# Expert borders of a routed SwiGLU: four scatter products and half a gathering in five PSUM banks, gates applied in the adding, float32 first products, groups of 32

## The chip, the cores and the metric

One core of a Trainium2 chip runs the whole program. The metric is device time in microseconds, median of several runs: 1387.23 us for the kernel before (three runs, 1385.8 to 1388.72). TensorE (PE) multiplies, VectorE (DVE) and ScalarE (ACT) do element work and move results out of PSUM, GpSimd (POOL) fills memory, SyncE (SP) issues the weight transfers.

## What is computed

A two-layer decoder trunk on 256 tokens of width 1024, all in float32. The second layer ends in eight expert SwiGLUs of hidden width 3584; each token goes to its two best experts.

```
logits = xf @ router
top_v, top_i = lax.top_k(logits, 2)
gates = softmax(top_v)
for e in range(8):
    y = y + gate[:, e] * ((silu(xf @ wg[e]) * (xf @ wu[e])) @ wd[e])
x = layer_norm(alpha * x + y)
```

The experts hold 8 x 44 MB of weights, which all pass through the chip once.

## The kernel before

Attention, the dense channel mixer and the router take the first 440 us or so and are not touched. The rest, function `moe`, goes through the experts in the order 3, 0, 1, 4, 5, 6, 7, 2 (ORDER). I number the places in this order e0 to e7.

**Expert bodies.** How many tokens an expert has is known only at run time. `tc.Switch` (line 1206) jumps, on every engine, into one of six bodies (CLASSES): up to 32 tokens, 64, 64 + 32, 128, 128 + 32, 128 + 128. A group of tokens that is computed together is called an arm (class `Part`). The trace shows by the shapes which bodies run: e0 32, e1 128 + 32, e2 64, e3 64 + 32, e4 64, e5 and e6 64 + 32, e7 32. A 128-token arm multiplies in three fp32r products of high and low halves (`mm3`, lines 920 to 922), for which ACT makes the high half (808) and DVE the low half (809) of tokens and weights. Smaller arms multiply in float32 (972 for gate and up, 1024 for down); a float32 matmul leaves two matmul records in the trace, an fp32r one leaves one.

**Weights.** The 42 blocks of 1 MB of an expert (16 gate, 14 up and down parts in turn) go through 17 half buffers. SP issues the transfer of block q + 17 when PE has finished block q (`done`, `fetch`, lines 852 and 857). SP too has six bodies, and goes through the jumps.

**Border between two experts.** In the body's end: `p_.end()` copies the results from PSUM to `hd` (1040, by DVE and ACT in turn), and `pick(0)` gathers the first half of the next expert's tokens, transposed, into `xg`: 8 matmuls with a 0/1 matrix `oh` (867) and a copy (1053, DVE). Then every engine jumps out of the body. The shared piece follows: `pick(1)` (8 matmuls, copy by ACT), a new `oh` that holds the gates (877, DVE), `scatter`, that is four matmuls (908) through the two `tr` banks of PSUM with four DVE adds into `acc` (911), and `shares_of`, which turns the gate matrix for the next expert (889, copy by ACT 890). Then every engine jumps into the next body. `ahead` gives a branch hint, to PE behind the last down product, to ACT behind pick(1), to DVE behind the gate matrix. For the tokens beyond 128 (e1's second arm) the body's start gathers them by full 128-column products (867, copies 1065), and its end scatters them (908, before `pick(0)`). PSUM has eight banks: four `acc`, two `mm`, two `tr`.

The order of instructions on an engine comes from a scheduler that follows data and the edges of `issue_after`; a body's `by_turns` sets how the two arms alternate.

## Time and profile before

| | |
|---|---|
| median of three runs | 1387.23 us |
| the profiled execution | 1387.88 us, its span 1386.2 us |
| PE busy | 1288.0 us (93%) |
| DVE, ACT busy | 483.6 us, 386.1 us |
| read from HBM | 424.32 MB |
| mean granted PE clock | 0.968 |

A row of the windows view gives a stretch of the span, its length, the busy time of each engine with the number of its records, the granted PE clock as a share of full speed, the busy share of the 16 DMA engines and GB/s. A row of the timeline gives start, length, engine, line, operation, output<-input, shape, number of records, and in brackets the engine's idle time before it with what ended it; `issue` means that no wait shows, as when an engine fetches code.

### The profile page before, as it was taken

How to read it: one execution, taken by the hardware profiler on the slowest of the kernel's cores; microseconds unless marked ns; L12 is line 12 of the kernel's file. 1: busy time of each engine (PE TensorE's matmuls, PEld its weight loads, DVE VectorE, ACT ScalarE, POOL GpSimd, SP SyncE). 2: the span in 40 equal slices, each digit the busy share in tenths (PEclk: the TensorE clock that was granted, in tenths of full speed). 3: DMA queues.
4: the chain of work that ended last, by engine and by line, in shares of the span. 5: the costliest groups of instructions: out<-in, count | busy, mean ns of one | idle time of the engine just before them, and what ended most of it. 6: DMA issues, size and time to landing. Idle time of an engine off the chain costs nothing.

```text
span 1386.2 us, 23696 instructions
## 1 busy us (share of the span) xinstructions
PE 1288.0 (93%) x10058; PEld 826.5 (60%) x10058; DVE 483.6 (35%) x786; ACT 386.1 (28%) x690; POOL 32.6 (2%) x51
## 2 busy tenths in 40 slices
PE   8999999999999966999999989998989998999874
PEld 7978999998877624677753333344343454334532
DVE  4688455566767203666751010001010001000102
ACT  5484444444664102556630000000000000000001
POOL 1010000000010000000000000000000000000000
PEclk9999999999999977999999999999999999999977
DMA  9427455554348899977757999999998999999796
GB/s 332 179 92 283 166 191 190 191 182 161 122 152 314 351 408 404 379 274 272 286 204 278 402 405 402 401 408 402 403 406 344 410 402 398 405 399 388 297 402 259
DMA packets 134056, 427.94 MB, mean 309 GB/s; under 512 B 8343, under 2 KB 14487, under 8 KB 133836
## 3 DMA queue, kind: packets, MB, share of 16 engines
q1 hardware_dynamic: 132764, 421.69, 79.2%
q0 software_dynamic: 1072, 3.71, 0.7%
q8 instruction: 90, 1.47, 0.4%
q14 instruction: 130, 1.06, 0.2%
HBM read 424.32 MB, written 1.06 MB: 307 GB/s over the span
## 4 chain that ended last, share of the span: by engine, by line
PE 81%; DMA 10%; issue 3%; DVE 2%; ACT 2%; SPq 1%; POOL 0%; DVEq 0%; ACTq 0%; POOLq 0%
PE mm L972 19%; PE acc L1024 13%; PE acc L972 7%; PE mm L324 4%; PE mm L326 4%; PE mm L325 4%; PE acc L324 4%; PE acc L325 4%; PE acc L326 3%; DMA piece<-in_moe_w_gate_dram 3%; DMA piece<-in_moe_w_up_dram 3%; DMA piece<-in_moe_w_down_dram 3%; PE tr L908 2%; PE mm L920 2%; PE tr L867 2%
## 5 line engine op out<-in xcount | busy, mean ns | idle before, releaser
L972 PE MATMUL mm<-piece,xg 128*64 128x512 f32 (+3 forms) x2048 | 290.5, 483 | 21.7 <-DMA piece<-in_moe_w_up_dram 10.4
L972 PEld LDWEIGHTS mm<-piece,xg 128*64 128x64 f32 (+1 forms) x2048 | 116.2, 129 | 174.6 <-issue 129.6
L1024 PE MATMUL acc<-piece,hT 128*32 128x256 f32 (+1 forms) x1752 | 199.9, 468 | 14.2 <-DMA piece<-in_moe_w_down_dram 13.3
L288 DVE TENSOR_TENSOR wl<-piece,wh 128x1024 fp32r<-128x1024 f32 (+4 forms) x128 | 140.2, 1102 | 89.2 <-ACT wh L286 86.6
L1024 PEld LDWEIGHTS acc<-piece,hT 128*32 128x32 f32 (+1 forms) x1752 | 75.2, 122 | 127.9 <-issue 85.4
L286 ACT ACTIVATE wh<-piece 128x1024 fp32r<-128x1024 f32 (+4 forms) x128 | 122.1, 960 | 86.2 <-PE acc L325 48.0
L324 PE MATMUL mm<-xTh,wl 128*128 128x256 f32 x448 | 126.6, 283 | 0.0
L325 PE MATMUL mm<-xTh,wh 128*128 128x256 f32 x448 | 125.7, 281 | 0.0
L326 PE MATMUL mm<-xTl,wh 128*128 128x256 f32 x448 | 125.7, 281 | 0.0
L990 ACT ACTIVATE hT<-tr 128x256 f32<-128x256 f32 (+2 forms) x43 | 17.9, 444 | 379.3 <-PE tr L997 301.0
L809 DVE TENSOR_TENSOR wl<-piece,wh 128x1024 fp32r<-128x1024 f32 (+1 forms) x88 | 97.8, 1127 | 48.3 <-ACT wh L808 32.1
L983 DVE TENSOR_TENSOR hd<-hd,mm 128x512 f32<-128x512 f32 (+2 forms) x34 | 20.0, 589 | 247.6 <-PE mm L972 247.5
L808 ACT ACTIVATE wh<-piece 128x1024 fp32r<-128x1024 f32 (+1 forms) x88 | 85.7, 983 | 58.0 <-PE mm L921 35.1
L983 DVE TENSOR_TENSOR h<-h,acc 128x256 f32<-128x256 f32 (+1 forms) x16 | 6.2, 388 | 233.6 <-PE acc L972 233.6
L324 PEld LDWEIGHTS mm<-xTh,wl 128*128 128x128 f32 x448 | 84.7, 189 | 0.2
L325 PEld LDWEIGHTS mm<-xTh,wh 128*128 128x128 f32 x448 | 84.5, 189 | 0.2
L326 PEld LDWEIGHTS mm<-xTl,wh 128*128 128x128 f32 x448 | 84.5, 189 | 0.0
L972 PE MATMUL acc<-piece,xg 128*32 128x256 f32 (+1 forms) x1472 | 74.7, 353 | 0.0
L972 PEld LDWEIGHTS acc<-piece,xg 128*32 128x32 f32 x1472 | 43.6, 110 | 36.5 <-issue 15.8
L981 ACT ACTIVATE hd<-mm 128x512 f32<-128x512 f32 (+2 forms) x34 | 17.5, 522 | 154.7 <-PE tr L997 109.9
L867 PE MATMUL tr<-oh,x_sb 128*128 128x128 f32 x288 | 41.6, 304 | 13.1 <-DVE oh L877 6.8
L908 PE MATMUL tr<-hd,sc 128*128 128x512 f32 (+1 forms) x64 | 40.3, 752 | 14.0 <-ACT xg L1053 10.3
(421 smaller groups left out, 1683.7 us busy)
## 6 DMA issues: line engine op xcount, KB each, us to landing
piece<-in_moe_w_gate_dram SPq DMA_DIRECT2D x108, 1024.0 KB, 16.9
piece<-in_moe_w_up_dram SPq DMA_DIRECT2D x104, 1024.0 KB, 18.3
piece<-in_moe_w_down_dram SPq DMA_DIRECT2D x104, 1024.0 KB, 14.9
piece<-in_ffn_w_gate_dram SPq DMA_DIRECT2D x5, 2048.0 KB, 7.9
piece<-in_ffn_w_up_dram SPq DMA_DIRECT2D x5, 2048.0 KB, 8.6
piece<-in_ffn_w_down_dram SPq DMA_DIRECT2D x5, 2048.0 KB, 11.2
piece<-in_w_in_dram SPq DMA_DIRECT2D x4, 2048.0 KB, 11.6
piece<-in_w_o_dram SPq DMA_DIRECT2D x4, 2048.0 KB, 8.4
```

What stands on the lines that cost most here:

```text
L286: hi = act.activation(h, src, AF.Copy)
L288: return hi, dve.tensor_sub(lo, src, h.bitcast(F32))
L324: pe.matmul(ps, lt[1], rt[0], start=start, stop=False)
L325: pe.matmul(ps, lt[0], rt[0], start=False, stop=False)
L326: pe.matmul(ps, lt[0], rt[1], start=False, stop=stop)
L808: act.activation(h, src, AF.Copy)
L809: dve.tensor_sub(lo, src, h.bitcast(F32))
L867: pe.matmul(tp[:, j * P:(j + 1) * P], src[:, t, (j0 + j) * P:(j0 + j + 1) * P], oh[:, t], start=t == 0, stop=t == 1)
L908: pe.matmul(ps, sc[:n, t * P:(t + 1) * P], hd[:n, hf], start=not total, stop=last or not total)
L920: pe.matmul(ps, lt[1], rt[0], start=start, stop=False)
L972: pe.matmul(ps[g * self.n:(g + 1) * self.n, :b], self.tokens(k), v[:, k - k0, g * w + j * b:g * w + (j + 1) * b], **at)
L1024: self.latest = pe.matmul(y[g * self.n:(g + 1) * self.n, c:c + w], self.hidden(j0 + j), v[:, j, i * w:(i + 1) * w], **at)
```

## The change

**Border.** The gates leave the 0/1 matrix: `oh` stays a 0/1 matrix, is turned inside the body behind `pick(0)` (`places_of`), and the gate is a factor in the adding (one `scalar_tensor_tensor` for each of the four sums). In the shared piece `bring` puts the four scatter products into four banks (two `tr`, two `acc`), `pick(1)` goes into an `mm` bank, and the four adds follow. `pick(0)` and the turning stand behind the last down product. Only PE gets a branch hint, behind them. e7, which no shared piece follows, makes its gate matrix in its own body.

**128-token arms.** The first four of eight row blocks of the first gate product use raw float32 `xg` and raw weights; tokens are split only when the fifth comes.

**Beyond 128.** With 32 such tokens, gathering, turning and scattering go in four groups of 32 rows or columns (`pick_few`, `scatter_few`), the gathering behind the first arm's first products; before the last down the arms' order is reversed, so that the small arm ends first.

```diff
-    def picked(src, oh, j0):
-
-        tp = bank("tr")
+    latest = {}
+
+    def picked(src, oh, j0, kind="tr"):
+
+        tp = bank(kind)
         for j in range(4):
             for t in range(2):
-                pe.matmul(tp[:, j * P:(j + 1) * P], src[:, t, (j0 + j) * P:(j0 + j + 1) * P], oh[:, t],
-                          start=t == 0, stop=t == 1)
+                ins = pe.matmul(tp[:, j * P:(j + 1) * P], src[:, t, (j0 + j) * P:(j0 + j + 1) * P], oh[:, t],
+                                  start=t == 0, stop=t == 1)
+        latest["pick"] = ins
...
-    def onehot(dst, e, off, weight):
+    def onehot(dst, e, off, weight, n=P):
 
         for t in range(2):
-            ins = dve.tensor_scalar(dst[:, t], iota[:, off:off + P], pos[:, t, e:e + 1], weight[:, t, e:e + 1],
-                                    op0=ALU.is_equal, op1=ALU.mult)
-        return ins
-
-    def shares(sc, e, off):
-
-        onehot(oh, e, off, gate)
-        shares_of(sc)
-
-    def shares_of(sc):
+            dve.tensor_scalar(dst[:, t].rearrange("p (g n) -> p g n", n=n),
+                              iota[:, off:off + n].unsqueeze(1).to_broadcast([P, P // n, n]),
+                              pos[:, t, e:e + 1], weight[:, t, e:e + 1], op0=ALU.is_equal, op1=ALU.mult)
+
+    def shares(sc, e, off, n=P):
+
+        onehot(oh, e, off, gate, n)
+        places_of(sc)
...
+    def bring(sc, e):
+
+        pss = [[bank(k) for _ in range(2)] for k in ("tr", "acc")]
+        for t in range(2):
+            for hf in range(2):
+                pe.matmul(pss[t][hf], sc[:, t * P:(t + 1) * P], hd[:, hf], start=True, stop=True)
+        return lambda: [dve.scalar_tensor_tensor(acc[:, t, HS[hf]], pss[t][hf], gate[:, t, e:e + 1], acc[:, t, HS[hf]],
+                                                 op0=ALU.mult, op1=ALU.add) for t in range(2) for hf in range(2)]
...
-                self.x = [part("xgh"), part("xgl")]
-                for k in range(0, 1024, 256):
-                    split_into(*[t[:, k:k + 256] for t in self.x], x[:, k:k + 256])
-                self.h, self.hT = h_all, [part("hT"), part("hTl")]
+                self.x, self.h, self.hT = None, h_all, [part("hT"), part("hTl")]
...
+                if self.parts and k < 4 and self.x is None:
+
+                    for j, ps in enumerate(self.ps):
+                        pe.matmul(ps, xg[:, k * P:(k + 1) * P], v[:, k - k0, j * 512:(j + 1) * 512], **at)
+                    continue
                 if self.parts:
+                    if self.x is None:
+                        self.x = [part("xgh"), part("xgl")]
+                        for q in (4, 6, 0, 2):
+                            split_into(*[t[:, q * P:(q + 2) * P] for t in self.x], xg[:, q * P:(q + 2) * P])
...
+    def pick_few(src, w, tmp, to):
+
+        n = 32
+        tp = bank("tr")
+        for t in range(2):
+            for g in range(4):
+                pe.matmul(tp[g * n:(g + 1) * n, :w], oh[:, t, :n], src[:, t, g * w:(g + 1) * w],
+                          start=t == 0, stop=t == 1)
+        act.copy(tmp[:, :w], tp[:, :w])
+        tp = bank("tr")
+        for c in range(0, w, P):
+            pe.transpose(tp[:, c:c + P], tmp[:, c:c + P], ident)
+        act.copy(to, tp[:, :w])
+
+    def scatter_few(sc, y):
+
+        n = 32
+        pss = [bank(k) for k in ("mm", "mm", "tr", "tr")]
+        for t in range(2):
+            for g, ps in enumerate(pss):
+                gs = slice(g * n, (g + 1) * n)
+                pe.matmul(ps[:, t * S:(t + 1) * S], sc[gs, t * P:(t + 1) * P], y[gs], start=True, stop=True)
+        for g, ps in enumerate(pss):
+            o = acc[:, :, g * S:(g + 1) * S]
+            dve.tensor_add(o, o, ps.rearrange("p (t n) -> p t n", t=2))
...
+                    if p_ in to_pick:
+                        to_pick.remove(p_)
+                        pick_beyond(p_)
...
+            shares(mine, e, 0)
...
+        turn[:] = parts[::-1]
         down(len(ws) - 1)
-        if not final:
-            ahead(i + 1, turn[0].latest)
         for p_ in beyond:
-            p_.end()
-            scatter(sc2, p_.n, total)
+            if few and not final:
+                act.copy(p_.h, p_.y[0][:, :S])
+                scatter_few(sc2, p_.h)
+            else:
+                p_.end()
+                if final:
+                    scatter(sc2, p_.n, total)
+                else:
+                    bring_weighted(sc2, p_.n)
...
+            return
+        with tc.issue_after(latest["down"].ins):
             pick(0)
+            turned = places_of(sc2)
+        ahead(i + 1, turned, latest["pick"])
...
-    def ahead(i, ins):
-
-        with tc.issue_after(ins.ins):
-            tc.switch_hint({ins.ins.engine: kinds[ORDER[i]]}, len(CLASSES), f"expert{i}")
...
+    def ahead(i, *behind):
+
+        with ExitStack() as s:
+            for ins in behind:
+                s.enter_context(tc.issue_after(ins.ins))
+            tc.switch_hint({pe.engine: kinds[ORDER[i]]}, len(CLASSES), f"expert{i}")
...
-            ahead(i, pick(1))
-            ahead(i, onehot(oh, e, 0, gate))
-            scatter(backs[(i - 1) % 2], P)
-            shares_of(backs[i % 2])
+            add = bring(backs[(i - 1) % 2], ORDER[i - 1])
+            pick(1, "mm")
+            add()
```

**PE at a border.** First the program before, from the end of a body (the last in the text, all end alike) through the shared piece to the first row of the next body for 32 tokens; line 867 is a pick, 908 the scatter, 889 the turning, 972 the gate product.

```order
L867 MATMUL tr<-oh,x_sb 128x128 x8
L1206 UNCONDITIONAL_BRANCH
L867 MATMUL tr<-oh,x_sb 128x128 x8
L908 MATMUL tr<-hd,sc_4567 128x512 x4
L889 MATMUL tr<-ident,oh 128x128 x2
L173 TENSOR_LOAD kind
L1206 SWITCH_STRIDE
L1206 ISA x2
L1194 BRANCH_PREFETCH_HINT
L972 MATMUL mm<-piece,xg 32x256 x32
```

Now the same place after; 869 is a pick, 893 the turning, 919 the scatter.

```order
L869 MATMUL tr<-oh,x_sb 128x128 x8
L893 MATMUL tr<-ident,oh 128x128 x2
L1249 SWITCH_STRIDE
L1249 ISA
L1249 BRANCH_PREFETCH_HINT
L1277 UNCONDITIONAL_BRANCH
L919 MATMUL tr<-hd,sc_4567 128x512 x2
L919 MATMUL acc<-hd,sc_4567 128x512 x2
L869 MATMUL mm<-oh,x_sb 128x128 x8
L173 TENSOR_LOAD kind
L1277 SWITCH_STRIDE
```

The turning has moved ahead of the jump, the hint behind it; the scatter stands before the second pick and uses four banks in place of two.

**PE at the start of the body for 128 + 32 tokens, e1.** Before: 867 gathers the tokens beyond 128, 920 to 922 are the three fp32r products, the first ones on row block 0.

```order
L867 MATMUL tr<-oh,x_sb 128x128 x16
L920 MATMUL mm<-wh,xgl 128x512
L921 MATMUL mm<-wh,xgh 128x512
L922 MATMUL mm<-wl,xgh 128x512
L920 MATMUL mm<-wh,xgl 128x512
L921 MATMUL mm<-wh,xgh 128x512
```

After: 976 are the float32 products of row blocks 0 to 3, 1078 and 1083 gather and turn in groups of 32, 930 to 932 are fp32r products of row block 4, 989 is the small arm.

```order
L976 MATMUL mm<-piece,xg 128x512 x8
L1078 MATMUL tr<-x_sb,oh 32x256 x8
L930 MATMUL mm<-wh,xgl 128x512
L931 MATMUL mm<-wh,xgh 128x512
L932 MATMUL mm<-wl,xgh 128x512
L1083 MATMUL tr<-ident,h_11742 128x128 x2
L930 MATMUL mm<-wh,xgl 128x512
L931 MATMUL mm<-wh,xgh 128x512
L932 MATMUL mm<-wl,xgh 128x512
L989 MATMUL acc<-piece,x_11741 32x256 x32
```

The gathering has moved behind eight products that need neither it nor a split.

**PE at the end of that body.** Before: 1024 is the small arm's last down, 908 the scatter of the tokens beyond 128.

```order
L922 MATMUL acc<-wl,hT 128x512
L1024 MATMUL acc<-piece,hT_11867 32x256 x7
L1177 SWITCH_STRIDE
L1177 ISA
L1177 BRANCH_PREFETCH_HINT
L908 MATMUL tr<-hd,sc_4566 128x512 x4
L867 MATMUL tr<-oh,x_sb 128x128 x8
L1206 UNCONDITIONAL_BRANCH
```

After: the large arm's fp32r products (932) come last, 1093 is the scatter in four groups.

```order
L932 MATMUL acc<-wl,hT 128x512
L1093 MATMUL mm<-h_11742,sc_4566 128x256 x2
L1093 MATMUL tr<-h_11742,sc_4566 128x256 x2
L1093 MATMUL mm<-h_11742,sc_4566 128x256 x2
L1093 MATMUL tr<-h_11742,sc_4566 128x256 x2
L869 MATMUL tr<-oh,x_sb 128x128 x8
L893 MATMUL tr<-ident,oh 128x128 x2
L1249 SWITCH_STRIDE
```

The small arm is now out of the way before the large arm's last products, and its scatter needs half the columns at a time.

More of the change, by code (lines that the diff above doesn't have):

```diff
@@ L901, in moe, with scatter @@
     backs = [mc.tile([P, S], F32, name=f"sc{n}") for n in range(2)]
-    def scatter(sc, n, total=None, last=False):
+    def scatter(sc, n, total, last=False):
         for t in range(2):
             for hf in range(2):
-                ps = total[t][hf] if total else bank("tr")
-                pe.matmul(ps, sc[:n, t * P:(t + 1) * P], hd[:n, hf], start=not total, stop=last or not total)
-                if not total:
-                    o = acc[:, t, HS[hf]]
-                    dve.tensor_add(o, o, ps)
+                pe.matmul(total[t][hf], sc[:n, t * P:(t + 1) * P], hd[:n, hf], start=False, stop=last)
+    def bring(sc, e):
[5 more added lines that the diff above has]
+                                                 op0=ALU.mult, op1=ALU.add) for t in range(2) for hf in range(2)]
     def split(src):
@@ L953, in tokens @@
             if self.off == P:
-                return self.x[:, k * self.n:(k + 1) * self.n]
+                c0 = k * P if self.n == P else k % 2 * P + k // 2 * self.n
+                return self.x[:, c0:c0 + self.n]
             return self.x[:, k * P + self.off:k * P + self.off + self.n]
@@ L1019, in down @@
                     for hf in range(2):
-                        self.latest = mm3(self.y[hf], self.hidden(j0 + j), [x[:, HS[hf]] for x in s], **at)
+                        latest["down"] = mm3(self.y[hf], self.hidden(j0 + j), [x[:, HS[hf]] for x in s], **at)
                     continue
@@ L1023, in down @@
                     y, g, c = self.result(i)
-                    self.latest = pe.matmul(y[g * self.n:(g + 1) * self.n, c:c + w], self.hidden(j0 + j),
-                                            v[:, j, i * w:(i + 1) * w], **at)
+                    latest["down"] = pe.matmul(y[g * self.n:(g + 1) * self.n, c:c + w], self.hidden(j0 + j),
+                                               v[:, j, i * w:(i + 1) * w], **at)
         def result(self, i):
@@ L1049, in moe, with pick, bring_weighted @@
                [(P, 0, True, (A, A), 2), (P, P, False, (TR, TR), 2)]]
-    def pick(q):
-        return (act.copy if q else dve.tensor_copy)(xg[:, q * 512:(q + 1) * 512], picked(x_sb, oh, 4 * q))
+    def pick(q, kind="tr"):
+        (act.copy if q else dve.tensor_copy)(xg[:, q * 512:(q + 1) * 512], picked(x_sb, oh, 4 * q, kind))
+    def pick_few(src, w, tmp, to):
[20 more added lines that the diff above has]
+            dve.tensor_add(o, o, ps.rearrange("p (t n) -> p t n", t=2))
+    def bring_weighted(sc, n):
+        for t in range(2):
+            for hf in range(2):
+                ps, o = bank("tr"), acc[:, t, HS[hf]]
+                pe.matmul(ps, sc[:n, t * P:(t + 1) * P], hd[:n, hf], start=True, stop=True)
+                dve.tensor_add(o, o, ps)
     def expert(i, cls, hT0, mine, sc2):
@@ L1059, in expert, with pick_beyond @@
         beyond = [p_ for p_ in parts if p_.off == P]
-        for p_ in beyond:
+        few = bool(beyond) and beyond[0].n < P
+        def pick_beyond(p_):
             onehot(oh, e, P, route.maskf)
-            w = 4 * p_.n
-            for src, j0, to in ((x_sb, 0, p_.x[:, :w]), (x_sb, 4, p_.x[:, w:2 * w]), (hd, 0, p_.hT[0][:, :w])):
+            if few:
+                pick_few(x_sb, 256, p_.h, p_.x)
+                if i == 0:
+                    pick_few(hd, P, p_.h, p_.hT[0][:, :P])
+                return
+            for src, j0, to in ((x_sb, 0, p_.x[:, :512]), (x_sb, 4, p_.x[:, 512:]), (hd, 0, p_.hT[0][:, :512])):
                 if src is x_sb or i == 0:
-                    act.activation(four(to), four(picked(src, oh, j0))[:, :, :p_.n], AF.Copy)
+                    act.activation(to, picked(src, oh, j0), AF.Copy)
+        to_pick = beyond[:]
         at_once = cls == 5
@@ L1105, in expert @@
         if beyond:
-            shares(sc2, e, P)
+            shares(sc2, e, P, beyond[0].n)
         if not final:
@@ L1135, in expert @@
             last_norm(total, gb)
-        else:
+            return
+        with tc.issue_after(latest["down"].ins):
             pick(0)
+            turned = places_of(sc2)
+        ahead(i + 1, turned, latest["pick"])
     def last_norm(z, gb):
@@ L1182, in moe @@
             onehot(oh, e, 0, route.maskf)
-            pick(0)
-            pick(1)
+            for q in range(2):
+                pick(q)
             hT0 = acc[:, 0, :512]
             act.activation(hT0, picked(hd, oh, 0), AF.Copy)
-            shares(backs[i % 2], e, 0)
+            places_of(backs[i % 2])
         else:
-            ahead(i, pick(1))
-            ahead(i, onehot(oh, e, 0, gate))
-            scatter(backs[(i - 1) % 2], P)
-            shares_of(backs[i % 2])
+            add = bring(backs[(i - 1) % 2], ORDER[i - 1])
+            pick(1, "mm")
+            add()
         for cls in tc.Switch(kinds[e], len(CLASSES), f"expert{i}"):
```

4 lines of the change are left out of this document (3 added, 1 removed).

## The prediction

> **What bounds the kernel now.** I read the page first, then the windows view cut at the borders between experts, then the timeline of three borders. The windows, from the start of the first expert to the last transfer:
>
> ```profile
> 527.50:550.00 22.50, 13.56 (x59) 10.49 (x59) 9.15 (x17) 6.15 (x12) 0.00 (x0) 0.75 1.03 402
> 550.00:716.70 166.70, 164.07 (x1280) 119.50 (x1278) 110.16 (x112) 96.30 (x113) 0.00 (x0) 1.00 0.79 299
> 716.70:734.50 17.80, 15.17 (x50) 8.22 (x50) 8.23 (x14) 2.28 (x5) 0.00 (x0) 0.81 0.18 63
> 734.50:812.50 78.00, 77.29 (x398) 30.59 (x398) 3.78 (x7) 4.03 (x8) 0.95 (x1) 1.00 0.98 383
> 812.50:824.10 11.60, 7.79 (x26) 3.85 (x26) 4.04 (x7) 1.55 (x3) 0.00 (x0) 0.85 1.02 404
> 824.10:939.70 115.60, 115.14 (x1125) 49.71 (x1125) 5.32 (x11) 6.71 (x17) 0.95 (x1) 1.00 1.03 404
> 939.70:952.30 12.60, 8.44 (x46) 5.12 (x42) 4.81 (x9) 1.69 (x4) 0.00 (x0) 1.00 1.03 404
> ...
> 1041.90:1157.10 115.20, 114.75 (x1121) 49.72 (x1125) 5.32 (x11) 6.71 (x17) 0.95 (x1) 1.00 0.99 387
> 1157.10:1171.60 14.50, 10.21 (x54) 5.70 (x44) 4.81 (x9) 1.69 (x4) 0.00 (x0) 0.88 1.03 392
> 1171.60:1287.20 115.60, 115.15 (x1125) 49.71 (x1125) 5.33 (x11) 6.71 (x17) 0.95 (x1) 1.00 1.02 398
> 1287.20:1300.40 13.20, 9.77 (x46) 5.74 (x42) 4.34 (x9) 1.31 (x3) 0.00 (x0) 0.87 0.54 200
> 1300.40:1372.00 71.60, 54.26 (x752) 27.62 (x753) 2.63 (x7) 3.72 (x11) 1.89 (x2) 0.83 0.98 382
> 1294.00:1302.00 8.00, 6.35 (x37) 2.94 (x41) 3.26 (x6) 0.80 (x2) 0.00 (x0) 0.79 0.11 40
> ```
>
> The rows are, in turn, border e0 to e1, the body of e1, border, e2, border, e3, border; left out are e4 and the border behind it, which read like e2 and its own but for full transfers; then e5, border, e6, border, e7 up to the last transfer. The last row is a piece of border e6 to e7. Two resources are full at once. PE is busy in nearly all of every body. The DMA share stands at 1.03, its ceiling here, from 734.5 to 1287, with two exceptions: e1 and its border at the end (0.79 and 0.18), where PE falls behind, all 17 buffers are full and transfers stop; and eight microseconds in border e6 to e7 (0.11). In e7 PE waits for data again (54.26 busy of 71.60), so the last transfer sets the end.
>
> So the rule for the sum: behind e1, time saved on PE shortens the span only where transfers stand still. Time saved in e1 and its two borders counts in full, since the transfers resume when e2's first block is done.
>
> **Part 1: border e0 to e1 and the start of e1.**
>
> ```profile
> 527.55 0.84 DVE L1040 COPY hd<-acc 32x256 f32<-32x256 f32 x2 [17.98 <-PE acc L1024]
> ...
> 528.54 3.53 PE L867 MATMUL tr<-oh,x_sb 128*128 128x128 f32 x16 [1.04 <-DVE hd L1040]
> ...
> 543.81 0.60 DVE L877 TENSOR_SCALAR oh<-iota,pos,maskf 128x128 f32<-128x128 bf16 x2 [5.97 <-issue]
> 544.06 1.33 ACT L808 ACTIVATE xgh<-xg 128x256 fp32r<-128x256 f32 x4 [6.16 <-issue]
> 544.30 5.94 PE L867 MATMUL tr<-oh,x_sb 128*128 128x128 f32 x32 [6.82 <-DVE oh L877]
> 544.50 1.43 DVE L809 TENSOR_TENSOR xgl<-xg,xgh 128x256 fp32r<-128x256 f32 x4
> 545.30 1.99 ACT L808 ACTIVATE wh<-piece 128x1024 fp32r<-128x1024 f32 x2
> 546.37 2.36 DVE L809 TENSOR_TENSOR wl<-piece,wh 128x1024 fp32r<-128x1024 f32 x2 [0.43 <-ACT wh L808]
> ...
> 555.62 3.66 PE L972 MATMUL acc<-piece,x 128*32 128x256 f32 x64
> 559.22 0.50 PE L920 MATMUL mm<-wh,xgl 128*128 128x512 f32 x1
> ...
> 564.56 0.39 PE L922 MATMUL mm<-wl,xgh 128*128 128x512 f32 x1
> ```
>
> The last down product ends at 527.5. DVE and ACT enter e1's body only after 5.97 and 6.16 us of `issue`, PE waits 6.82 us for them, gathers for 5.94 us, and at 565.0, 37.5 us after the down product, has done eight row blocks of the large arm and the small arm's first 64 records.
>
> Between 559.22 and 564.95 stand 24 fp32r records, four row blocks: 1.36 us a row block at the 0.227 from one start to the next, and 5.4 for four.
>
> What the new order does, in us behind the down product, needs the pace of float32 products, which the last scatter in the chain of waits gives (four records in 1.73 us, 0.43 each, two to a product of 512 columns, so 0.87):
>
> ```profile
> 1373.86 1.73 PE acc L908 x4
> ```
>
> and the prices of a border, here e5 to e6 in the timeline, with a multiply-and-add of the same size from the end of the program:
>
> ```profile
> 1159.61 0.69 DVE L1053 COPY xg<-tr 128x512 f32<-128x512 f32 x1 [0.21 <-PE tr L867]
> 1160.45 2.02 PE L867 MATMUL tr<-oh,x_sb 128*128 128x128 f32 x16 [0.88 <-DVE xg L1053]
> ...
> 1165.55 0.60 DVE L877 TENSOR_SCALAR oh<-iota,pos,gate 128x128 f32<-128x128 bf16 x2 [5.24 <-issue]
> ...
> 1169.43 0.69 DVE L911 TENSOR_TENSOR acc<-acc,tr 128x512 f32<-128x512 f32 x1 [1.57 <-PE tr L908]
> 1170.45 0.38 PE L889 MATMUL tr<-ident,oh 128*128 128x128 f32 x2
> ...
> 1171.63 1.94 PE L972 MATMUL mm<-piece,xg 128*64 128x512 f32 x8 [0.79 <-issue]
> ...
> 1375.66 0.74 DVE L1165 SCALAR_TENSOR_TENSOR acc<-mm,mv,piece 128x512 f32<-128x512 f32 x1
> ```
>
> PE: pick(0) 3.5 (the clock is halved here, as for the pick that took 3.53 at 528.54 where it takes 2.02 at 1160.45) and the turning 0.8 (0.38 at full clock) end at 4.3; the wait for the copy of pick(0), 0.69, ends by 4.8; four scatter products 3.5, to 8.3; pick(1) 2.0, to 10.3; the jump about 0.5 (nearest row: 0.79 idle before the gate product), to 10.8. Eight float32 products follow at 0.87: 17.7. They cost 7.0 us where 24 fp32r ones take 5.4, 1.6 more, but need no split. DVE leaves the body at 4.7, needs 5.0 to come out (nearest row 5.24), adds four times 0.74 to 12.7, enters by 18.7 (5.97), makes the one-hot to 19.3. PE gathers in groups in about 0.9 (a quarter of the columns of 32 records at 5.94 us): 20.2. ACT enters at 17.1, splits tokens (1.33) and three weight blocks (1.0 each) to 21.5, then copies the gathered rows. DVE's low halves of tokens (1.43) and of row block 4 (1.2) are ready at 21.9. PE then goes through block 4, the turning, the small arm's 64 records (3.66) and blocks 5 to 7 (three times 1.36) and is at 31.2 where it was at 37.5. **Saved: 6.3 us.** If the groups of 32 went one after the other it would be 2 us less; if the two jumps took 3 us less without the work that now stands before them, 3 more.
>
> **Part 2: the end of e1.**
>
> ```profile
> 716.77 0.41 DVE L1040 COPY hd<-acc 32x256 f32<-32x256 f32 x1 [3.05 <-PE acc L1024]
> 717.63 5.68 PE L908 MATMUL tr<-hd,sc 32*128 32x512 f32 x8 [0.95 <-ACT hd L1040]
> ...
> 723.24 3.48 PE L867 MATMUL tr<-oh,x_sb 128*128 128x128 f32 x16
> ...
> 734.57 2.80 PE L972 MATMUL mm<-piece,xg 128*64 128x512 f32 x12 [0.90 <-issue]
> ...
> 736.59 2.07 SPq L857 DMA_DIRECT2D piece<-in_moe_w_down_dram  x2
> ```
>
> From the last down product (716.7) to e2's first product take 17.9 us, of them 5.68 for the scatter beyond 128; SP's transfers resume at 736.59, when PE has finished e2's first block. After: eight products of 256 columns on four row groups. If the groups run side by side, as the four column groups at 555.62 do (64 records in 3.66 us, 0.057 each where a record of 256 columns alone takes half of 0.43), they take 0.9 us, one after the other 3.4. I take 0.9, the nearer kind of row, and keep 3.4. DVE's four adds (0.69 each) end at 3.8; pick(0) needs a `tr` bank that the third frees: 3.1 to 5.1; copy to 5.9; scatter to 9.5, pick(1) to 11.5, jump, 12.0. **Saved: 5.9 us** (3.4 at the other end).
>
> **Part 3: the borders behind.** With nothing beyond 128 a border takes 2.9 (pick(0) 2.0, its copy 0.69, the wait), scatter 3.5, pick(1) 2.0, jump 0.5: 8.9 us from the last down product, where the windows show 12.6, 14.5 and 13.2 behind bodies of 64 + 32, and 11.6 behind those of 64, whose down phase held pick(0), 2.0 us, as well. That is 3.7, 5.6, 4.3 and twice 4.7 saved on PE. What hid nothing before and is covered now: the four adds leave PE's path. DVE ends them at about 11 and its jump by 17, ACT is in the body by 15; the first silu is due at 16 behind a body of 64 (about 7 us of products behind the start). Up to e6's end PE thus arrives 18.7 us earlier against transfers that run without a gap. So the buffers are no longer all full there, and the idle stretch from 1294 to 1302 goes: 8.0 x (1.03 - 0.11) / 1.03 = **7.1 us**. The rest, 11.6 us, I put at nothing: transfers cover it. If that cover went, it would come as a gain, not a loss. The dent in e5 (0.99 of 1.03, 4.5 us) I leave as it is, since SP's jump lies in it.
>
> e7's own gate matrix and its turning (0.7 and 0.4 us) lie where PE waits for data, and cost nothing.
>
> **Sum.** 6.3 + 5.9 + 7.1 = 19.3 us. The profiled execution took 1387.88 us, 1.7 more than its span; the median is 1387.23. Forecast: 1387.2 - 19.3 = **1367.9 us**.
>
> [...]
>
> **Rivals.**
> 1. *PE's jump is no longer covered.* PE paid 0.79 to 0.90 us with a hint far ahead. If the fetch takes the 5 to 6 us of the other engines and starts late, a border loses up to 4 us: parts 1 and 2 fall from 12.2 to about 6, and 7.1 to about 5. Gain 11: 1376. Or only the gap at e6 stays, because SP's own jump makes it: 19.3 - 7.1, 1375. Together 0.3.
> 2. *The dent in e5 closes too* and DVE's jump into e1 is shorter without the gate matrix: 19.3 + 4.5 + 2, 1361. 0.12.
> 3. *Slower: DVE and ACT pay much more without hints.* One mechanism, at the entry of every body: if an entry takes X instead of 6, e1's start loses X - 6, e2's start X - 13.6 (two products' length of cover), the others likewise. The gains of 19.3 are gone at X of about 19; at 24 it is 18 + 10 lost against 19, 1396, and more when the borders behind turn up. For it speaks only that the hints go. Against: SP never had a hint, and its dearest pair of jumps, out and in, fits into 13.6 us less a transfer's issue (1057.14 to 1070.74 below). 0.05.
> 4. *No change*, because the transfers alone set the end: only if parts 1 and 2 fail too. 0.03.
>
> ```profile
> 1057.14 2.28 SPq L857 DMA_DIRECT2D piece<-in_moe_w_down_dram  x1
> ...
> 1070.74 0.38 SPq L857 DMA_DIRECT2D piece<-in_moe_w_down_dram  x1
> ```
>
> **Numbers.** The forecast, 1363 to 1372, has 0.5. The range takes in rival 2 and rival 1 and the bounds of parts 1 and 2: 1358 to 1377. A measurement of this kernel can tell about 0.2% (2.8 us). Faster by more 0.90 (the forecast, rival 2 and 0.28 of rival 1), within 0.05 (rival 4 and the tail of rival 1), slower 0.05.
>
> **What would show it.** After: no `issue` wait of PE over 1 us at a border; first gate product of e1 about 11 us behind the down product, of e2 12, elsewhere 9; DMA share 1.03 from e2's start to the last transfer, without the stretch of 0.11. Wrong if PE waits for code, if ACT's or DVE's entry grows beyond 7 us, or if the span falls by the whole of PE's 35 us, which would mean that transfers were not at their ceiling.

## The result, and the profile after

The changed kernel took **1377.78 us** (median of four runs, 1374.49 to 1377.93) against 1387.97 for the kernel before in the same comparison (four runs, 1385.8 to 1389.37): ratio 0.9922, 95% interval 0.9902 to 0.9943. It is faster, by 10 us where I forecast 19. The profiled execution took 1377.88 us, its span 1376.2.

The windows view of after, cut at the same places: border e0 to e1, e1, border, e2, border, e3, border; then border e5 to e6, e6, border e6 to e7, e7; the last row is the stretch of border e6 to e7 in which transfers stand still.

```profile
524.70:538.20 13.50, 10.32 (x42) 7.36 (x43) 4.53 (x7) 1.11 (x3) 0.00 (x0) 0.77 1.03 403
538.20:709.00 170.80, 167.09 (x1293) 118.28 (x1291) 110.87 (x117) 97.53 (x119) 0.00 (x0) 1.00 0.82 314
709.00:721.90 12.90, 10.29 (x61) 7.62 (x60) 6.23 (x10) 0.97 (x2) 0.00 (x0) 0.87 0.21 81
721.90:797.70 75.80, 75.18 (x384) 27.54 (x383) 3.09 (x6) 4.62 (x9) 0.95 (x1) 1.00 0.98 384
797.70:805.90 8.20, 7.54 (x42) 5.31 (x42) 1.88 (x3) 0.97 (x2) 0.00 (x0) 1.00 1.03 401
805.90:922.60 116.70, 116.28 (x1127) 49.77 (x1126) 7.71 (x16) 7.44 (x19) 0.95 (x1) 1.00 1.02 402
922.60:936.90 14.30, 9.81 (x44) 6.18 (x44) 4.38 (x6) 0.97 (x2) 0.00 (x0) 0.76 1.02 401
1142.50:1156.00 13.50, 9.14 (x42) 5.97 (x43) 4.38 (x6) 0.97 (x2) 0.00 (x0) 0.87 1.02 401
1156.00:1272.70 116.70, 116.28 (x1127) 49.78 (x1127) 5.49 (x13) 7.44 (x19) 0.95 (x1) 1.00 1.03 404
1272.70:1288.80 16.10, 10.54 (x46) 6.46 (x48) 4.98 (x8) 1.55 (x3) 0.00 (x0) 0.79 0.43 160
1288.80:1363.00 74.20, 57.10 (x757) 28.71 (x758) 3.08 (x7) 3.87 (x11) 1.89 (x2) 0.82 0.94 369
1276.00:1292.00 16.00, 11.58 (x85) 6.86 (x89) 3.61 (x6) 0.59 (x1) 0.00 (x0) 0.79 0.28 92
```

The borders fall into two kinds. Behind the 64-token body e2 (and e4, 8.24 as well) a border takes 8.2 us. Behind bodies of 32 and 64 + 32 it takes 13.5, 14.3, 13.5 and 16.1, the last three hardly less than before or more (12.6, 14.5 and 13.2). The idle stretch at e6 to e7 is not gone: 16.0 x (1.03 - 0.28) / 1.03 = 11.7 us are lost where 7.1 were. The waits view names what is new. PE's waits for code (`issue`), in all, times and longest; before, then after:

```profile
PE mm L972 <- issue: 3.3, 4, 0.9
```

```profile
PE tr L919 <- issue: 16.7, 4, 4.7
```

Four times PE stands, 16.7 us together, ahead of the first scatter product (919), that is behind the jump *out of* the body. The timeline of after at borders e0 to e1 and e3 to e4:

```profile
523.60 1.08 PE L1041 MATMUL acc<-piece,hT 128*32 128x256 f32 x8
524.61 3.45 PE L869 MATMUL tr<-oh,x_sb 128*128 128x128 f32 x16
527.90 0.38 PE L893 MATMUL tr<-ident,oh 128*128 128x128 f32 x2
531.46 3.41 PE L919 MATMUL tr<-hd,sc 128*128 128x512 f32 x4 [3.18 <-issue]
534.71 1.88 PE L919 MATMUL acc<-hd,sc 128*128 128x512 f32 x4
536.42 1.95 PE L869 MATMUL mm<-oh,x_sb 128*128 128x128 f32 x16
538.21 7.11 PE L976 MATMUL mm<-piece,xg 128*128 128x512 f32 x16
543.03 0.60 DVE L880 TENSOR_SCALAR oh<-iota,pos,maskf 128x128 f32<-128x128 bf16 x2 [5.65 <-issue]
544.16 1.33 ACT L808 ACTIVATE xgh<-xg 128x256 fp32r<-128x256 f32 x4 [5.17 <-issue]
545.25 1.07 PE L1078 MATMUL tr<-x_sb,oh 128*32 128x256 f32 x16
...
557.31 0.39 PE L932 MATMUL mm<-wl,xgh 128*128 128x512 f32 x1
```

```profile
924.28 0.25 PEld L893 LDWEIGHTS tr<-ident,oh 128*128 128x128 f32 x2
924.39 0.38 PE L893 MATMUL tr<-ident,oh 128*128 128x128 f32 x2
...
929.26 3.75 PE L919 MATMUL tr<-hd,sc 128*128 128x512 f32 x4 [4.49 <-issue]
```

A second cost stands behind the wait, a lower clock: the four records at 531.46 take 3.41 us, the next four 1.88, and the granted clock is 0.53 from 531.4 to 534.6 and 1.00 from 534.6 to 536.5; the four at 929.26 take 3.75, at a granted clock of 0.50 from 929.2 to 933.0.

**What the trace's own records add.** Below the level of the views, the trace of each run holds three more kinds of record: PE's branches with their durations, PE's hints, and the packets of q8, the instruction queue whose packets go with PE's counts. In the page of after that queue is

```profile
q8 instruction: 94, 1.54, 0.5%
```

94 packets of 16,384 bytes. Inside a body one comes for about every 256 PE instructions, if a float32 matmul is counted as four instructions (two records, each with its weight load) and an fp32r matmul or a transpose as two: in e3 of after nine, from 808.72 to 911.63, for 2307 instructions. I call 256 instructions a page of code. In after these packets come at nearly the same counts in e3, e5 and e6, wherever the body lies in the code (by the records, the last of the nine 2126, 2126 and 2142 instructions behind the branch into the body); I conclude that a body begins on a new page. The branch out of e3 began at 923.09 and lasted 6.01 us; while it lasted, one packet came, from 926.58 to 927.66. In the kernel before, the same branch took 0.34, and none came. The table gives, for each body, by how many instructions it runs over its last full page (negative: stays short of it), and the duration of the branch out of it:

| | e0 | e3 | e5 | e6 | e2 | e4 |
|---|---|---|---|---|---|---|
| before, over by | -4 | -1 | -1 | -1 | 46 | 48 |
| before, exit us | 0.32 | 0.34 | 0.50 | 0.33 | 0.50 | 0.41 |
| after, over by | 1 | 3 | 3 | 3 | 53 | 53 |
| after, exit us | 6.09 | 6.01 | 5.71 | 6.18 | 1.08 | 1.34 |

So a theory of mine, which no record shows directly and the runs below test: the page that the exit jumps to is asked for only when the body's last page is entered, and comes about 6 us later. Before, the bodies of 32 and 64 + 32 tokens ended 4 and 1 instructions short of a page, so the last page was entered 252 or more instructions ahead. The turning (two transposes, four instructions) and the rest of the change put them 1 and 3 instructions into a new page, which is entered right at the exit.

### The profile page after: what moved, and what is told of

The parts are those of the page before. It is cut to its first block, busy times and chain, and to the rows that moved or that the text cites. A ratio compares the mean times of both kernels' runs of the same rounds, so it can differ in the third digit from the quotient of the medians.

```text
span 1376.2 us, 23535 instructions
## 1 busy us (share of the span) xinstructions
PE 1285.6 (93%) x10046; PEld 818.4 (59%) x10046; DVE 475.0 (35%) x766; ACT 381.8 (28%) x686; POOL 32.6 (2%) x51
## 4 chain that ended last, share of the span: by engine, by line
PE 81%; DMA 11%; issue 3%; ACT 2%; DVE 2%; SPq 1%; POOL 1%; ACTq 0%; POOLq 0%; DVEq 0%
PE mm L989 18%; PE acc L1041 12%; PE acc L989 7%; PE mm L326 4%; PE mm L324 4%; PE mm L325 4%; DMA piece<-in_moe_w_down_dram 4%; PE acc L324 4%; PE acc L325 4%; PE acc L326 4%; DMA piece<-in_moe_w_gate_dram 3%; DMA piece<-in_moe_w_up_dram 3%; PE mm L930 2%; PE mm L931 2%; PE mm L932 2%
## 5 line engine op out<-in xcount | busy, mean ns | idle before, releaser
L989 PE MATMUL mm<-piece,xg 128*64 128x512 f32 (+3 forms) x2048 | 290.7, 483 | 19.4 <-DMA piece<-in_moe_w_up_dram 10.8
L989 PEld LDWEIGHTS mm<-piece,xg 128*64 128x64 f32 (+1 forms) x2048 | 113.3, 129 | 174.7 <-issue 126.4
L1041 PE MATMUL acc<-piece,hT 128*32 128x256 f32 (+1 forms) x1752 | 204.1, 472 | 13.5 <-DMA piece<-in_moe_w_down_dram 12.7
L809 DVE TENSOR_TENSOR wl<-piece,wh 128x1024 fp32r<-128x1024 f32 (+1 forms) x84 | 92.9, 1123 | 46.4 <-ACT wh L808 34.1
L808 ACT ACTIVATE wh<-piece 128x1024 fp32r<-128x1024 f32 (+1 forms) x84 | 81.3, 979 | 54.6 <-PE mm L931 33.1
L1057 DVE COPY hd<-acc 32x256 f32<-32x256 f32 (+2 forms) x16 | 8.3, 519 | 113.1 <-PE acc L1041 67.1
L324 PE MATMUL acc<-wh,xTl 128*128 128x512 f32 (+2 forms) x128 | 46.5, 364 | 0.0
```

What stands on the lines that cost most here:

```text
L324: pe.matmul(ps, lt[1], rt[0], start=start, stop=False)
L808: act.activation(h, src, AF.Copy)
L809: dve.tensor_sub(lo, src, h.bitcast(F32))
L989: pe.matmul(ps[g * self.n:(g + 1) * self.n, :b], self.tokens(k), v[:, k - k0, g * w + j * b:g * w + (j + 1) * b], **at)
L1041: latest["down"] = pe.matmul(y[g * self.n:(g + 1) * self.n, c:c + w], self.hidden(j0 + j), v[:, j, i * w:(i + 1) * w], **at)
```

## The experiments

Each run is compared with the kernel before on the same chip (1387.5 to 1388.9 us there). Edits are to the changed kernel, but for the first.

**x1: the kernel before with eight PE instructions more.** In the bodies of 32 and 64 + 32 tokens one block is transposed four more times; the result is not used.

```diff
-                for j in range(nb):
+                for j in [*range(nb), *[0] * again]:
...
-            p_.turned(ws[-1])
+            p_.turned(ws[-1], 4 if cls in (0, 2) and p_ is parts[0] else 0)
```

> The kernel before, with eight more PE instructions (the first of the last turned blocks is turned four times more into the same place, about 0.4 us) in the bodies for 32 and for 64 + 32 tokens, which brings those bodies from 5 to 6 instructions below a multiple of 256 to 3 to 6 above one; nothing else. Page theory (PE's code comes in pages of 256 instructions; a body that runs over into a new page has the next page on its way when it jumps, and the jump waits for it): the exit branch of PE grows from 0.3 to 0.5 us to about 6 us behind e0, e3, e5 and e6, the borders behind e3, e5 and e6 get 3 to 4 us longer, 1390 to 1394 us against 1387.5. Hint theory (the branch hint directly in front of the exit branch holds it up): the exit branches stay at 0.3 to 0.5 us and the time within 1 us of before.

Measured: 1403.97 us (1403.34 to 1408.19, 4 runs), ratio 1.0123 [1.0099, 1.0146]. (The expectation gives 5 to 6 instructions short; by the count of the table it was 4 and 1.) Twenty transposes of some 0.1 us each (x10 shows 2.6 us for 24) made the old kernel nearly 16 us slower. Its exits, now 4 and 7 instructions over: 6.18, 6.12, 6.02, 6.15 us, as the page theory had it. The time rose by 10 us more than that theory expected: the branch into e5 took 6.36, and its border 19.2 us instead of 12.9, while the borders behind e3, e5 and e6 grew by 2.1, 0.7 and 2.3. The waits view of this run:

```profile
PE tr L867 <- issue: 17.8, 4, 5.0
```

The old kernel had the same edge one step away; neither hints nor the order at the border were touched here.

**x2: the turning goes back behind the jump.** It is done in the shared piece, between scatter and pick(1), with an `mm` bank.

```diff
             pick(0)
-            turned = places_of(sc2)
-        ahead(i + 1, turned, latest["pick"])
+        ahead(i + 1, latest["pick"])
...
             add = bring(backs[(i - 1) % 2], ORDER[i - 1])
+            places_of(backs[i % 2], "mm")
```

> The changed kernel with the turning (two transposes, four PE instructions) moved from the body's end into the shared piece, between scatter and second pick, through an mm bank; the hint stays directly in front of the exit branch. Page theory: the body for 32 tokens ends below its page boundary again, that for 64 + 32 at its last instruction; exit branches 0.3 to 1 us in place of 6, borders behind e0, e3, e5, e6 of 9 to 10 us, 1366 to 1371 us. If the count is off by one, only e0's exit gets short and the time is 1374 to 1377. Hint theory: exit branches stay at 6 us, 1376 to 1379 us.

Measured: 1368.09 us (1367.39 to 1373.87, 4 runs), 0.9866 [0.9838, 0.9895]. Bodies 3 short and exactly full; exits 0.32 to 0.33; border e0 to e1 9.29 us; exits and time as the page theory expected. But the branches *into* e2, e4 and e6 now take 3.79, 5.93 and 5.95 us: the shared piece, 58 instructions here, lies across a page edge at these three places (by a count in which one constant is fitted; over all runs it fails three times, in x8, x9 and x10, where the piece ends a few instructions beyond the edge and the entry costs 0.3 to 1.2). The entry into e7, 2.21 here, has no such edge and stays unexplained.

**x3 and x4: is it the hint?** x3 puts PE's hint ahead of pick(0), with the same number of instructions; x4 is x2 with the hint behind the first scatter product.

```diff
+        ahead(i + 1, latest["down"])
         with tc.issue_after(latest["down"].ins):
             pick(0)
-            turned = places_of(sc2)
-        ahead(i + 1, turned, latest["pick"])
+            places_of(sc2)
```

> The changed kernel with PE's hint directly behind the last down product, ahead of pick(0) and the turning, about 2.4 us earlier; the number of instructions is the same. Hint theory: the exit branch waits 2.4 us less or not at all, 1370 to 1375 us. Page theory: the exit branches of e0, e3, e5 and e6 stay at 5.5 to 6.5 us, 1376 to 1379 us.

```diff
+            ahead(i, latest["bring"])
+            places_of(backs[i % 2], "mm")
```

> As the kernel with the turning in the shared piece, and PE's hint there too, behind the first scatter product: the bodies end 5 to 10 instructions below the page boundary. Both theories: exit branches 0.3 to 0.5 us. The hint stands only 4 to 5 us ahead of the entry branch, which may wait 1 to 2 us, under the 16 queued records of pick(1): borders of 9 us, 1365 to 1370 us. If the late hint isn't covered, borders of 10 to 12 and 1370 to 1374 us.

Measured: x3 1374.9 us (1372.16 to 1376.34, 4 runs), exits of e0, e3, e5, e6 still 6.17, 6.15, 6.12, 6.70: where the hint stands doesn't make the wait (the time lies in the range of the hint theory, but its interval, 0.9878 to 0.9918, overlaps that of the changed kernel). x4, expected at 1365 to 1374, took 1387.45 us (1383.15 to 1389.99, 10 runs), 0.9993 [0.9982, 1.0004]: exits 0.32, but five of seven entries cost 5.8 to 6.2; the two where transfers stand still cost 0.82 and 0.33. Its waits view:

```profile
PE mm L991 <- issue: 19.3, 4, 5.6
PE mm L978 <- issue: 4.6, 1, 4.6
```

With the hint ahead of the exit, as in after, the entries took 0.40 to 1.58 us but for e7's (3.44); with the hint behind it, in x4, the whole gain of the change is lost.

**x5 and x6: hint early, and hints for ACT and DVE again.** x5 is x2 with x3's hint; x6 adds the hints of ACT and DVE in the shared piece that the change dropped.

> The kernel with the turning in the shared piece, and PE's hint ahead of pick(0), directly behind the last down product. Page theory with a second half (a hint is fetched only if it comes some time ahead of the exit branch; x2, whose hint stood 0.1 us ahead of it, paid 3.8 to 5.9 us at three entries): exit branches 0.3 to 0.5 us, entry branches 0.3 to 0.7, borders behind e1, e3, e5 of 9 to 11.5 us in place of 14, e2's start 2 to 3 us earlier than in x2, 1362 to 1367 us. If the entries stay at 4 to 6 us, the hint's place isn't their cause: 1366 to 1370 us.

```diff
-            pick(1, "mm")
-            add()
+            for ins in (pick(1, "mm"), add()[-1]):
+                with tc.issue_after(ins.ins):
+                    tc.switch_hint({ins.ins.engine: kinds[e]}, len(CLASSES), f"expert{i}")
```

> As x5, with the hints of ACT and DVE put back into the shared piece, behind pick(1)'s copy and behind the last add. If they are worth nothing, as the prediction has it: entries of DVE and ACT into e1 at 5 to 6 us of issue as without, the time within 1.5 us of x5. If dropping them cost something: e1's first split 2 to 5 us earlier, and the time 2 to 5 us below x5.

Measured: x5 1376.53 us (1373.61 to 1382.41, 4 runs), 0.99 [0.987, 0.993], where 1362 to 1370 was expected; x6 1380.61 (1376.21 to 1381.41, 5 runs), 0.9934 [0.9912, 0.9956], not to be told apart from x5. The three entries that were dear in x2 stay so with the early hint (3.36, 6.02 and 6.43 us), so it is not a late hint that makes them dear. In x5 the exits of the 64-token bodies, which run 50 over, went from about 1 to 6.08 and 6.02 us (in x3, 53 over, to 1.59 and 4.53). Their fetch is seen only after the exit has begun. My guess, which no record shows directly: the early hint comes between the entering of the last page and the start of that fetch and puts it off, as if one page could be pending at a time. Two exits with the hint as early don't fit and stay open: e2's in x3 (1.59) and e4's in x6 (1.72). ACT's and DVE's hints bought nothing: their idle times at e1's entry were 5.30 and 4.44 us without and 5.65 and 4.93 with.

**x7 and x8: the two other parts.** x7 is x5 with the float32 first products undone (and the tokens split in their old order); x8 is x5 with tokens beyond 128 scattered by full products instead of groups of 32.

```diff
-                if self.parts and k < 4 and self.x is None:
+                if self.parts and k < 0 and self.x is None:
```

```diff
-            if few and not final:
+            if False:
```

> As x5, with the first four row blocks of a 128-token arm's first product in split fp32r again, so that PE waits at e1's start for the entry and the splits of ACT and DVE. By the prediction's step the eight float32 products stand in the time that PE would wait: e1's state (eight row blocks and the small arm's first 64 records) comes 4 to 6 us later, 1.6 us of it given back by the cheaper products, and the whole is 3.5 to 6 us slower than x5, since e1 counts in full.

> As x5, with the tokens beyond 128 scattered by four products of 512 columns and four adds through two tr banks, as before, in place of the groups of 32. If the groups run side by side (0.9 us), the border e1 to e2 gets 4 to 5.5 us longer and the time 4 to 5.5 us; if they run one after the other (3.4 us), 2 to 3 us.

Measured: x7 1391.12 us (1384.24 to 1396.84, 10 runs), 14.6 us above x5 where 3.5 to 6 were expected. From e0's to e1's last down product it takes 186.7 us, x5 180.7: the float32 start is worth 6.0, the size that was expected. In the rest of its loss stands the page edge again: its 64 + 32 bodies grew from 2304 instructions, exits 0.42 to 0.45, to 2305, exits 6.17, 6.14, 6.71. One instruction, 6 us.

x8: 1365.78 us (1360.2 to 1370.46, 4 runs), 10.8 us under x5 where 2 to 5.5 us more were expected. Its whole scatter takes 3.88 us, and pick(0) starts 3.74 us behind the last down product:

```profile
708.47 2.05 PE L869 MATMUL tr<-oh,x_sb 128*128 128x128 f32 x16
```

In x5 pick(0) starts 3.03 us behind the last down product: the groups of 32 in the scatter are worth some 0.7 us here, not the 2 to 5.5 expected. Border e1 to e2 takes 12.27 us in x8 and 15.54 in x5, but 2.27 of the difference is PE's wait at x5's entry and 1.6 a pick(0) at a granted clock of 0.54 (3.68 us). The groups were sized by the 5.68 us that the whole scatter took before, at a granted clock of 0.66. x8 gained elsewhere. Its body for 128 + 32 tokens, which runs in e1 alone but stands in the code of every expert, got shorter, which by the fitted count of x2 moved shared pieces off the page edges: the entries of e4 and e6 fell from 6.02 and 6.43 to 0.49 and 0.50 us, borders e3 to e4 and e5 to e6 from 13.46 and 13.86 to 8.46.

**x9: x8 with the hint back at the body's end** (the edit is against x8).

```diff
-        ahead(i + 1, latest["down"])
         with tc.issue_after(latest["down"].ins):
             pick(0)
+        ahead(i + 1, latest["pick"])
```

> Edit: the turning behind the jump, tokens beyond 128 scattered whole, PE's hint back at the body's end, behind pick(0); the instruction counts are those of the run with the whole scatter (e0's body 3 instructions short of a page of 256, the 64 + 32 bodies exactly full, the 64 bodies 50 beyond one), only the hint has moved by 3.9 us towards the jump. Theory (PE's code comes in pages of 256 instructions; the page that the exit jumps to is asked for when the body's last page is entered, and a hint that is issued before that takes its place): the exits behind the 64 bodies e2 and e4, 6.06 and 4.67 us with the early hint, fall to the 1.1 to 1.3 us that they take in the changed kernel, all others stay at 0.3 to 0.5, no shared piece's entry waits over 1 us except e3's and e5's up to 1.6; borders e2 to e3 and e4 to e5 8.5 us, all others as with the early hint (8.5, 9.1, 12.3). Time 1357 to 1364 us against 1365.8 with the early hint. Rival 1 (the early hint is harmless and the 6 us are transfers in the way): borders e2 to e3 and e4 to e5 stay at 13.5 and 10.8, time 1364 to 1370. Rival 2 (transfers set the end of all this already): borders as the theory says, time within 2 us of 1365.8.

Measured: 1365.62 us (1365.02 to 1370.17, 5 runs), 0.9837 [0.9821, 0.9854]. Exits behind e2 and e4 fell to 1.05 and 1.27, all borders behind e2 to 8.46, as the theory said, and the time stayed: its rival 2. In the profiled executions the border e2 to e3 is 5.0 us shorter than in x8, and e4's body, which waits for transfers, 5.0 longer (84.58 against 79.61): what was saved on PE at a place where transfers run without a gap was given back there.

**x10 and x11: more work, so that the page is entered earlier.** The changed kernel itself with useless transposes added, 24 in the bodies for 32 and 64 + 32 tokens (x11: 40 in that for 32), and some in a body that never runs, which only shifts the code behind it.

```diff
-            p_.turned(ws[-1])
+            p_.turned(ws[-1], {0: 24, 2: 24, 3: 20}.get(cls, 0) if p_ is parts[0] else 0)
```

> Edit: the changed kernel with work added: 24 more transposes of one block in the last turning of the bodies for 32 and for 64 + 32 tokens (48 PE instructions, 2.4 us at the 0.1 us that four of them took per transpose in the run on the kernel before), and 20 in the body for 128 tokens, which never runs, so that the shared pieces lie against the pages as they did. The bodies now run 49 (e0) and 51 (e3, e5, e6) instructions into a new page instead of 1 and 3. Theory (the page that the exit needs is fetched from the moment that the body's last page is entered, about 6 us): the page is entered some 5 us before the exit instead of just ahead of it, as in the 64 bodies, which run 53 over; so the exits fall from 6.09, 6.01, 5.71 and 6.18 us to 1 to 2 us. Borders e0 to e1 9 us, e3 to e4 9.5 to 10, e5 to e6 9 to 10, e6 to e7 11 to 12 (its entry still waits 3.4, as the piece still straddles); bodies 2.4 us longer. By the run without the turning in the body, where 5.7 us less at each of the four exits gave 9.7 us, the net 2.4 us at each gives about 4: 1371 to 1376 us, faster than the changed kernel although it does more. Rival (the 6 us are the price of a jump with a late hint, whatever the counts): exits stay at 6, bodies 2.4 longer, 1380 to 1387.

> Edit: as the run with 24 more transposes, but 40 more in the body for 32 tokens (e0), 24 in that for 64 + 32, and 4 in the unused body for 128, which puts every shared piece within one page. The question is e0's exit, which stayed at 6.01 us with 24 more while e3's, e5's and e6's fell to 0.41 to 0.58. Theory (one pending fetch at a time): there e0 entered its last page about 1.2 us before the hint for the next entry, and a page needs 3.6 us from the asking to the start of its fetch, so the hint threw the exit's fetch away; with 81 instructions in the last page instead of 49 the page is entered one more down product earlier, some 2 us or more, or ahead of a wait for a transfer, the fetch starts before the hint, and the exit takes 1 to 2 us (fetch in the packets starting before the hint). Border e0 to e1 9 us instead of 13.7; the exit behind e6 stays below 0.6 and its entry falls from 1.15 to 0.4. e0's extra 1.6 us lie where PE waits for transfers. Time 1360 to 1365 us. Rival (e0's exit costs 6 us for another reason, since its body is short): exit 6 us, border 13.5 to 14, time 1364 to 1367.

Measured: x10 **1364.93 us** (1362.9 to 1371.57, 6 runs), 0.982 [0.9807, 0.9833]; x11 **1362.73 us** (1360.71 to 1366.04, 5 runs), 0.9827 [0.9811, 0.9843]. x10 was expected at 1371 to 1376, x11 at 1360 to 1365. Both beat the changed kernel by about 1% although PE does 2.6 us more in each of those bodies (119.28 against 116.66 in e3). In x10 the exits of e3, e5 and e6 (51 over) fell to 0.45, 0.41 and 0.58; that of e0 (49 over) stayed at 6.01: the hint at 526.19 came before any fetch for the exit, which began at 529.81. In x11, with e0 81 over, a fetch began at 522.04, the hint came at 523.23, and the exit took 1.22. Windows of x11, border e0 to e1, e1, border, e2, border, e3, border; then border e6 to e7 and the twelve microseconds around its gap:

```profile
522.80:531.70 8.90, 8.24 (x45) 6.12 (x44) 1.99 (x4) 1.11 (x3) 0.00 (x0) 0.92 1.02 402
531.70:703.80 172.10, 167.10 (x1293) 118.26 (x1291) 113.04 (x121) 97.53 (x119) 0.00 (x0) 1.00 0.86 326
703.80:715.10 11.30, 8.69 (x58) 6.06 (x58) 6.22 (x10) 0.97 (x2) 0.00 (x0) 1.00 0.23 92
715.10:790.90 75.80, 75.18 (x384) 27.49 (x383) 3.08 (x6) 4.61 (x9) 0.95 (x1) 1.00 0.98 386
790.90:799.20 8.30, 7.64 (x46) 5.40 (x44) 1.81 (x3) 0.96 (x2) 0.00 (x0) 1.00 1.02 399
799.20:918.40 119.20, 118.78 (x1151) 52.28 (x1150) 7.78 (x16) 7.43 (x19) 0.95 (x1) 1.00 1.02 402
918.40:926.70 8.30, 7.64 (x45) 5.40 (x44) 2.12 (x4) 0.96 (x2) 0.00 (x0) 1.00 1.03 403
...
1265.20:1273.40 8.20, 7.54 (x42) 5.32 (x42) 1.98 (x3) 0.96 (x2) 0.00 (x0) 1.00 0.82 309
```

```profile
1268.00:1280.00 12.00, 11.96 (x148) 7.38 (x152) 3.33 (x6) 0.97 (x2) 0.00 (x0) 1.00 0.72 257
```

Every border is down to 8.2 to 8.9 us (e1 to e2 11.3), PE's clock in those that were long is 0.92 to 1.00 where it was 0.76 to 0.87, and the gap at e6 to e7 loses 12.0 x (1.03 - 0.72) / 1.03 = 3.6 us instead of 11.7. One by-effect isn't the page: e0's body ends 1.9 us earlier than in the changed kernel from the same start, and its granted clock from 505 to 520 us is 0.93 where it was 0.61. The transposes keep PE busy there; that they raise the clock is not tested apart.

x8, x9, x10 and x11 can't be told apart by their intervals. The lowest median, x11's, is 15 us under the changed kernel and 25 under the one before.

## Why the prediction was wrong

The profiled executions, from the start of the span, in us (rounded):

| | forecast | after | x11 |
|---|---|---|---|
| e0's last down product earlier by | 0 | 2.8 | 4.7 |
| from there to e2's first product, saved (parts 1 and 2) | 12.2 | 9.9 | 14.7 |
| from there to the end, saved (part 3) | 7.1 | -2.7 | 7.7 |
| sum | 19.3 | 10.0 | 27.2 |

**The step that failed** is in part 3: "pick(1) 2.0, jump 0.5", with it "Up to e6's end PE thus arrives 18.7 us earlier" and "the idle stretch from 1294 to 1302 goes". I costed the jump into the next body, and took the jump out of a body, 0.3 to 0.5 us in the trace of before, as free. That it was so short hung on 1 and 4 instructions; in after it took 5.7 to 6.2 us at four borders. PE arrived at e7 with an exit of 6.18 and an entry of 3.44 us, so the gap in the transfers grew to 11.7 us, and the first half of the last scatter ran at half clock (four records in 3.75 us, 1.96 before; the granted clock was 0.52 from 1360.5 to 1364). With the exits short again (x11) the term is 7.7, near the 7.1 forecast, but in part by luck: the stretch still loses 3.6 us, so it gave 3.5, and the other 4.2 come from smaller differences that I did not take apart. The waits view of SP at this border, in before (1286 to 1304), after (1272 to 1292) and x11 (1264 to 1280), shows why it does not go whole; each row gives the waits in all, their number and the longest:

```profile
SPq L857 <- PE mm L972: 6.3, 3, 5.6
```

```profile
SPq L857 <- PE mm L989: 9.6, 3, 8.9
```

```profile
SPq L857 <- PE mm L989: 1.4, 3, 0.7
```

SP's wait for PE, 5.6 us before and 8.9 in after, is nearly gone in x11. What is left is SP's own two jumps: in x11 it branches out of e6's body at 1265.63, and its first record in e7's body is at 1273.79. The second half of rival 1 ("only the gap at e6 stays, because SP's own jump makes it") thus fits this remainder. Nor did PE get 18.7 us ahead: counted from e2's first product, e6's last down product came 2.0 us earlier in after and 2.7 in x11, since in e4's body PE caught up with the transfers and waited for them (76.6 us before, 80.7 and 83.4).

**Rival 1** gave 1376, close to the result, by luck, for another reason: it put the wait at the entry and on the hint's late place. Entries cost 0.40 to 1.58 us in after with that hint, but for the one at e7; the exits went with the count: in x3, with the same counts and the hint elsewhere, they stayed at 6.12 to 6.70; in x10, with other counts, three of the four fell to 0.41 to 0.58. The prediction did name PE waiting for code as what would prove it wrong.

**Part 1** was to save 6.3 and saved 4.5: the state forecast at 31.2 us behind the down product was reached at 557.70 - 524.68 = 33.0. The border took 13.53 instead of 10.8 (the exit, and the scatter at half clock behind it); the rest went 0.9 better than forecast. Float32 products 7.11 us (forecast 7.0), the gathering in groups 1.07 (0.9): right. Entries of DVE and ACT 5.65 and 5.17 us (taken: 5.97): right, and rival 3 is out.

**Part 2** was to save 5.9 and saved 5.0: 12.89 us instead of 12.0. The eight products of the groups ran side by side as taken (16 records from 708.93 to 710.08). pick(0) waited, as forecast, for a bank that DVE's adds free, and began 3.0 us behind the down product (forecast 3.1):

```profile
PE tr L869 <- DVE acc L1096: 2.0, 1, 2.0
```

```profile
712.03 3.60 PE L869 MATMUL tr<-oh,x_sb 128*128 128x128 f32 x16 [1.96 <-DVE acc L1096]
```

It took 3.60 us instead of 2.0: the granted clock was 0.54 there. In x11 the same instructions behind the same wait ran at a granted clock of 1.00, pick(0) took 2.05 and the border 11.34; in x10 the border took 14.29, at 0.76. So one trace fixes this term only to some 1.5 us either way.

**Part 3's borders**: 8.24 behind the 64-token bodies, forecast 8.9: right. Behind the others the forecast held only where the exits were cured (8.24 in x11).

**Not foreseen**: e0 itself starts earlier (first gate product 464.68 before, 462.19 after). Of these 2.5 us, 0.9 lie ahead of everything that was changed (the first pick starts at 456.63 and 455.72), and over the runs of the changed code e0 starts between 461.9 and 465.9. So the 2.8 us in the first row of the table are in part chance, and not shown to come from the change.

**Behind e1, PE's time counts only at gaps**: confirmed by x9. It has a limit: in x1 the borders behind e2 grew by 11 us together, and the time rose by 16. There the DMA share of e6 is 0.96 where it was 1.02, and that of the border ahead of it 0.94 instead of 1.03: PE had fallen so far behind that transfers stopped where they ran before.

**Page edges in the middle of a body** show no such cost: in e3 of after, which crosses eight of them before the last, PE is busy 116.28 of 116.70 us. The last one, just ahead of the exit, stands beside a branch of 6.01 us (0.34 before).

## What to carry to other kernels

Where a program jumps between bodies, count the instructions of the engine that sets the time (here PE) against the code page seen in its trace (here 256 instructions) before you cost an edit. Here one instruction more at a body's end took exits from 0.42 to 0.45 us to 6.14 to 6.71 (x7), and eight more in the bodies for 32 and 64 + 32 tokens made the kernel before nearly 16 us slower (x1). A jump that took 0.3 to 0.5 us in the trace of before took 5.7 to 6.2 after the change; ask what covers it and by how little. What cured it here was moving work past the jump (x2, exits of 0.32 to 0.33 us) or adding some ahead of it (x10, three of four exits at 0.41 to 0.58). Look at each branch's own duration.
